# Seven products for the gate and up matmuls of 12 of 22 feature tiles

## The chip, the cores and the metric

One NeuronCore of a Trainium2 chip runs the whole kernel. Its engines work side by side and wait for each other by semaphores: TensorE (PE; PEld is its weight load), VectorE (DVE), ScalarE (ACT), GpSimd (POOL), and SP, whose queue issues most DMA transfers. The metric is the device time of one execution in microseconds; a lower number is better. SBUF is the on-chip memory that all engines read, PSUM the banks that TensorE writes its sums to; a bank holds 128 x 512 numbers of 32 bits.

## What is computed

A decoder trunk of two layers over 512 tokens of width 1024, in 32-bit floats. Each layer is a half-step feed-forward, three gated token mixers side by side, and a second half-step feed-forward, each between RMS norms:

```python
def _swiglu(t, w_gate, w_up, w_down):
    return (jax.nn.silu(t @ w_gate) * (t @ w_up)) @ w_down
for l in range(DEPTH):
    f = _swiglu(_rmsnorm(h, ffn1_pre_g[l]), ffn1_w_gate[l], ffn1_w_up[l], ffn1_w_down[l])
    h = h + 0.5 * _rmsnorm(f, ffn1_post_g[l])
    ...                       # stick-breaking, forgetting and memory attention, gated and merged
    f = _swiglu(_rmsnorm(h, ffn2_pre_g[l]), ffn2_w_gate[l], ffn2_w_up[l], ffn2_w_down[l])
    h = h + 0.5 * _rmsnorm(f, ffn2_post_g[l])
```

The gate and up weights are 1024 x 2816, that is 22 feature tiles of 128 columns; the down weights are 2816 x 1024. There are four feed-forwards, which the tile names call a0, c0, a1 and c1 (the digit is the layer); the mixing stages are b0 and b1.

## The kernel before, in words

**Arithmetic.** A 32-bit product is made of three products of a faster, shorter format. `split` writes a high part of a tile with ScalarE (L188, or L191 with a scale) and the remainder with VectorE (L189, L192); `mm3` (L214 to L216) adds high x high, high x low and low x high into one PSUM bank. So each weight tile costs one DMA, one ScalarE cast and one VectorE subtraction ahead of its matmuls, all in units of 128 x 1024 numbers (512 KB).

**Queue of jobs.** The work for TensorE is a list of jobs, each with the weight units that it needs. When a job begins, its units and the next four are loaded (`load`, `load_ahead`, `AHEAD = 4`); the raw tiles go through a ring of two buffers (tag `raw`), the high and low parts through four each (`wh`, `wl`). `weave` lets TensorE work through jobs while a chain of other steps (normalization, attention heads) waits for its own results; the waits in the attention heads are written as numbers of us (`W_SB0`, `W_SB1`, `W_MORE`). The framework's scheduler then orders the instructions on each engine, and assigns buffers and semaphores; each engine executes its own list strictly in order.

**A feed-forward** (`ffn`). `src.us` is the normalized input, transposed so that features lie on partitions, in high and low parts, for 512 tokens. For feature tiles two at a time: `gates` and `ups` multiply the weight columns (held in the array) with all 512 tokens (streamed), eight k tiles each, so 2 x 2 x 8 x 3 = 96 matmuls of 512 columns for a pair; `hidden` applies SiLU with ScalarE and multiplies with VectorE (L652). The first pair is computed in two halves of the tokens (`halved`, L677 to L680), because the last tokens are normalized late. PSUM has four banks of tag `mm` for these and four of tag `z`.

**The down projection** of the first 16 feature tiles is made with Strassen's seven products instead of eight block products (in Winograd's form, so that sums can be built up step by step), in two chunks of eight tiles: `first_factor` builds sums of blocks of the hidden values, `BlockUnit` loads blocks of the weights and builds their sums on VectorE (L335 to L346) in tiles that `Keep` holds, `product` runs one of the seven (24 matmuls, activations held in the array, weights streamed, output token-major) and copies or adds the PSUM sums into the output tiles (L753, L755). These products are queued one at a time between the gate and up jobs of later tiles. The last six tiles are done in full in `down`, which ends with the residual addition (L598), the next normalization (L605) and the transposes into the next `us` (L615) token tile by token tile.

**The residual stream** `h` is four tiles of 128 x 1024 of tag `o` (eight buffers). It stays in SBUF through a feed-forward; in the mixing stage it is written to a DRAM tensor `hsave` and read back in time for the residual addition.

Of the kernel before, what the change touches and what calls it, by code (L numbers as in the profile page):

```python
# [17 lines left out]
P = 128  # L18
# [4 lines left out]
def kernel(  # L23
# [264 lines left out]
    class BlockUnit(Unit):  # L288
# [19 lines left out]
        def block(self, dst, b):  # L308
            r = (b[0] * self.rows + self.k0) * P
            return nc.sync.dma_start(dst, self.src[r:r + self.nk * P, b[1] * self.ncol:(b[1] + 1) * self.ncol]  # L310
                                     .rearrange("(k p) c -> p k c", p=P))
# [14 lines left out]
        def load(self):  # L326
# [7 lines left out]
            elif self.n == 2:  # L334
                nc.vector.tensor_tensor(t, t, self.raw[:], ALU.subtract)  # L335
                src = t
            elif self.n == 3:
                nc.vector.tensor_tensor(t, b, t, ALU.subtract)
                src = t
            elif self.n == 4:  # L340
                src = b
            elif self.n == 5:
                nc.vector.tensor_tensor(b, b, self.raw[:], ALU.subtract)
# [289 lines left out]

    def ffn(l, src, wg, wu, wd, dst, name, spare, aside=None):
# [7 lines left out]
        tags = ["q"] * 2 + ["o"] * 4  # L642
        act = lambda k, c=FULL: quad_act(src.us)(k, c)

        def hidden(f, pg, pu):
            s = tmp(f"s{name}_{f}")
            nc.scalar.activation(s[:], pg[:], AF.Silu)
            if f < NC * FC:
                i = 2 * f // FC
                if f % (FC // 2) == 0:  # L650
                    hr[i] = stile([P, FC // 2, S], ("k", "tri")[f // FC], f"hr{name}_{i}", F32)
                nc.vector.tensor_tensor(hr[i][:, f % (FC // 2)], pu[:], s[:], ALU.mult)  # L652
                return
            nc.vector.tensor_tensor(s[:], pu[:], s[:], ALU.mult)
            hid[f] = blk(tags[f - NC * FC], f"hid{name}_{f}")
            split(hid[f][:, 0], hid[f][:, 1], s[:])
            if f == NF - 1:
                tc.keep_in_program_order(nc.scalar.preload_act_table_set("natural_log_exp_and_others"))

        def halved(f, ug, uu, half):  # L660
            if half == 0:
                st["p"] = [pbank("mm", f"p{x}{name}_{f + m}") for x in "gu" for m in range(2)]
            else:
                Q.hold, Q.pinned = False, True
                Q.load_ahead()
                Q.pinned = False
            c = HALVES[half]
# [38 lines left out]
        def first_factor(ci, n):  # L706

            a = lambda i, j: hr[2 * ci + j][:, :, HALVES[i]]
# [4 lines left out]
            s = st.get(("s", ci))  # L713
            if n == 2:
                nc.vector.tensor_tensor(s, a(1, 0), a(1, 1), ALU.add)
            elif n == 3:
                nc.vector.tensor_tensor(s, s, a(0, 0), ALU.subtract)
            elif n == 4:
                nc.vector.tensor_tensor(s, a(0, 1), s, ALU.subtract)
            elif n == 5:  # L720
                nc.vector.tensor_tensor(s, a(0, 0), a(1, 0), ALU.subtract)
            src = (a(0, 0), a(0, 1), s, s, s, s, a(1, 1))[n]
            split(h, l, src, scale=-1.0 if n == 6 else None)
# [7 lines left out]
        def product(ci, n, uns):  # L731
            if n == 0 and ci == 0:
                dst.begin()
            if n < 6:
                first_factor(ci, n + 1)
# [21 lines left out]
        def products(ci):  # L757

            def make(i, k0):

                if ci == 0:
                    return stile([P, 2, S], "qo"[i], f"bt{name}_{i}_{k0}", F32)[:]
# [5 lines left out]
            for n in range(7):  # L768
# [4 lines left out]
        for f in range(0, NF, 2):  # L773
            ug = wpair(wg[l], ND, f * P, f"g{name}_{f}")
            uu = wpair(wu[l], ND, f * P, f"u{name}_{f}")
            if f == 0:
# [4 lines left out]
                Q.add([], lambda ug=ug, uu=uu: halved(0, ug, uu, 1), src.ready(range(NT)))  # L781
                marks["first"] = len(Q.jobs)
                continue
            ci = f // FC if f % FC == FC - 2 and f < NC * FC else None
            Q.add(ug, lambda f=f, ug=ug: gates(f, ug))
            for one in todo:
                Q.add(*one)
                break
            if ci is not None:
                Q.add([], lambda ci=ci: iter(first_factor(ci, 0) or ()))  # L790
# [767 lines left out]
```

## Time and profile before

| | |
|---|---|
| time of the kernel, median of 3 runs | 2432.78 us (2432.51 to 2433.62) |
| the profiled execution's own time | 2433.56 us |
| its span, first to last instruction | 2431.8 us |
| granted TensorE clock, mean | 0.999 |
| TensorE busy | 2420.0 us, 11832 matmuls |
| VectorE busy | 1549.7 us |
| ScalarE busy | 1173.6 us |
| GpSimd busy | 78.0 us |
| moved by DMA | 280.46 MB |
| feed-forward a0, from its first matmul to the mixing stage | about 12 to 390 us |
| mixing stage b0 | about 390 to 867 us |
| feed-forward c0 | 867 to 1220 us |
| feed-forward a1 | 1220 to 1596 us |
| mixing stage b1 | 1596 to 2073 us |
| feed-forward c1 and the end | 2073 to 2431 us |

The busy time of TensorE overstates its work, because the profile shows each matmul longer than the distance to the next one; distances between starts are the better measure. A group's row gives line, engine, operation, output and inputs by the program's names, the shape, the count, then total busy us and mean ns, then the idle time of the engine just before and what ended it. A row of the timeline gives start in us, duration in us, engine, line, operation and tiles.

### The profile page before, as it was taken

How to read it: one execution, taken by the hardware profiler on the slowest of the kernel's cores; microseconds unless marked ns; L12 is line 12 of the kernel's file. 1: busy time of each engine (PE TensorE's matmuls, PEld its weight loads, DVE VectorE, ACT ScalarE, POOL GpSimd, SP SyncE). 2: the span in 40 equal slices, each digit the busy share in tenths (PEclk: the TensorE clock that was granted, in tenths of full speed). 3: DMA queues.
4: the chain of work that ended last, by engine and by line, in shares of the span. 5: the costliest groups of instructions: out<-in, count | busy, mean ns of one | idle time of the engine just before them, and what ended most of it. 6: DMA issues, size and time to landing. Idle time of an engine off the chain costs nothing.

```text
span 2431.8 us, 30227 instructions
## 1 busy us (share of the span) xinstructions
PE 2420.0 (100%) x11832; PEld 2044.3 (84%) x11832; DVE 1549.7 (64%) x2183; ACT 1173.6 (48%) x1895; POOL 78.0 (3%) x130
## 2 busy tenths in 40 slices
PE   9999999999999999999999999999999999999998
PEld 8888888888888898888898888888888888888887
DVE  5364677678776654646654546776777866445466
ACT  4333365577655543333433333555775655333333
POOL 0000000001110000000000000000011100000000
PEclk9999999999999999999999999999999999999999
DMA  4334445222223433333424344442232234333433
GB/s 140 116 127 130 133 162 156 70 74 74 87 63 121 138 104 113 130 127 124 156 87 136 109 144 132 159 136 67 73 89 77 79 130 132 94 130 111 141 114 129
DMA packets 234643, 280.46 MB, mean 115 GB/s; under 512 B 8682, under 2 KB 180994, under 8 KB 234500
## 3 DMA queue, kind: packets, MB, share of 16 engines
q1 hardware_dynamic: 234400, 278.50, 35.9%
q8 instruction: 93, 1.52, 0.3%
q14 instruction: 50, 0.41, 0.1%
q0 software_dynamic: 96, 0.03, 0.0%
q10 hardware_dynamic: 4, 0.00, 0.0%
HBM read 272.20 MB, written 6.29 MB: 115 GB/s over the span
## 4 chain that ended last, share of the span: by engine, by line
PE 95%; DVE 2%; ACT 1%; DMA 0%; issue 0%; DVEq 0%; ACTq 0%
PE pg L214 3%; PE pg L215 3%; PE pg L216 3%; PE pgc L215 3%; PE puc L215 3%; PE pgc L214 3%; PE pgc L216 3%; PE puc L214 3%; PE puc L216 3%; PE pga L214 3%; PE pga L215 3%; PE pga L216 3%; PE pdc L214 3%; PE pdc L215 3%; PE pdc L216 3%; PE pda L216 3%
## 5 line engine op out<-in xcount | busy, mean ns | idle before, releaser
L214 PE MATMUL pg<-us_a,wh_wg 128*128 128x512 f32 x384 | 150.6, 392 | 0.0
L216 PE MATMUL pg<-us_a,wl_wg 128*128 128x512 f32 x384 | 149.6, 390 | 0.0
L215 PE MATMUL pg<-us_a,wh_wg 128*128 128x512 f32 x384 | 149.6, 390 | 0.0
L214 PE MATMUL pgc<-us_b,wh_gc 128*128 128x512 f32 x320 | 124.5, 389 | 0.0
L215 PE MATMUL pgc<-us_b,wh_gc 128*128 128x512 f32 x320 | 124.5, 389 | 0.0
L216 PE MATMUL pgc<-us_b,wl_gc 128*128 128x512 f32 x320 | 124.5, 389 | 0.0
L214 PE MATMUL puc<-us_b,wh_uc 128*128 128x512 f32 x320 | 124.5, 389 | 0.0
L215 PE MATMUL puc<-us_b,wh_uc 128*128 128x512 f32 x320 | 124.5, 389 | 0.0
L216 PE MATMUL puc<-us_b,wl_uc 128*128 128x512 f32 x320 | 124.5, 389 | 0.0
L189 DVE TENSOR_TENSOR wl_uc<-raw_uc,wh_uc 128x1024 fp32r<-128x1024 f32 x44 | 53.9, 1225 | 106.6 <-ACT wh_uc L188 106.6
L189 DVE TENSOR_TENSOR wl_ua<-raw_ua,wh_ua 128x1024 fp32r<-128x1024 f32 x44 | 53.8, 1225 | 99.1 <-ACT wh_ua L188 99.1
L188 ACT CAST wh_uc<-raw_uc 128x1024 fp32r<-128x1024 f32 x44 | 46.3, 1052 | 88.5 <-PE pgc L215 37.5
L189 DVE TENSOR_TENSOR wl_gc<-raw_gc,wh_gc 128x1024 fp32r<-128x1024 f32 x40 | 48.8, 1224 | 62.1 <-ACT wh_gc L188 61.8
L216 PE MATMUL pda<-wh_da,ala 128*128 128x512 f32 x224 | 87.1, 389 | 0.0
L214 PE MATMUL pda<-wh_da,aha 128*128 128x512 f32 x224 | 87.1, 389 | 0.0
L215 PE MATMUL pda<-wl_da,aha 128*128 128x512 f32 x224 | 87.1, 389 | 0.0
L214 PE MATMUL pdc<-wh_dc,ahc 128*128 128x512 f32 x224 | 87.1, 389 | 0.0
L215 PE MATMUL pdc<-wl_dc,ahc 128*128 128x512 f32 x224 | 87.1, 389 | 0.0
L216 PE MATMUL pdc<-wh_dc,alc 128*128 128x512 f32 x224 | 87.1, 389 | 0.0
L189 DVE TENSOR_TENSOR wl_ga<-raw_ga,wh_ga 128x1024 fp32r<-128x1024 f32 x40 | 48.8, 1224 | 58.9 <-ACT wh_ga L188 58.8
L188 ACT CAST wh_ua<-raw_ua 128x1024 fp32r<-128x1024 f32 x44 | 46.1, 1051 | 82.0 <-PE pga L215 35.8
L216 PEld LDWEIGHTS pg<-us_a,wl_wg 128*128 128x128 f32 x384 | 72.1, 188 | 15.2
(468 smaller groups left out, 7145.4 us busy)
## 6 DMA issues: line engine op xcount, KB each, us to landing
raw_da<-in_ffn_w_down_dram SPq DMA_DIRECT2D x58, 512.0 KB, 3.7
raw_dc<-in_ffn_w_down_dram SPq DMA_DIRECT2D x58, 512.0 KB, 3.3
raw_wg<-in_w_gate_dram SPq DMA_DIRECT2D x48, 512.0 KB, 3.5
raw_ga<-in_ffn_w_gate_dram SPq DMA_DIRECT2D x44, 512.0 KB, 3.7
raw_ua<-in_ffn_w_up_dram SPq DMA_DIRECT2D x44, 512.0 KB, 3.7
raw_gc<-in_ffn_w_gate_dram SPq DMA_DIRECT2D x44, 512.0 KB, 3.6
raw_uc<-in_ffn_w_up_dram SPq DMA_DIRECT2D x44, 512.0 KB, 3.6
raw_wo<-in_w_out_dram SPq DMA_DIRECT2D x24, 512.0 KB, 3.2
```

The costliest lines, as they stand in the source:

```text
L188: both = [nc.scalar.copy(h_ap, src)]
L189: make = lambda: nc.vector.tensor_tensor(l_ap, src, h_ap.bitcast(F32), ALU.subtract)
L214: nc.tensor.matmul(pt, lh, rh, start=start, stop=False, skip_group_check=free)
L215: nc.tensor.matmul(pt, lh, rl, start=False, stop=False, skip_group_check=free)
L216: nc.tensor.matmul(pt, ll, rh, start=False, stop=stop, skip_group_check=free)
```

## The change

In each feed-forward, feature tiles 2 to 5, 6 to 9 and 14 to 17 (`TG`) are no longer computed by `gates` and `ups`. For a group of four, the gate columns and the up columns (512 each) are put side by side as one matrix of 1024 x 1024, and the product with the tokens (512 x 1024) is made with the same seven products (`group`, `gate_up`): tokens are held in the array, weights streamed, and the result is token-major. The order of the seven is 0, 2, 3, 4, 5, 1, 6, now in the down projection too.

- The sums of weight blocks for these groups are made on GpSimd (`self.engine`); those of the down projection stay on VectorE.
- The sums of blocks of the input are made once per feed-forward (`sums`): two by GpSimd during the first half of the first pair, the others by VectorE in the second half, and split into high and low parts (`parts_of`).
- After the seven products, SiLU and multiplication are done token-major, and `feature_major` transposes the result back with TensorE (16 transposes a group), queued behind the second job of the next group or behind the next gate job.
- The hidden values for the down projection lie in eight tiles of two feature tiles each (`pair`, `HR`), so `first_factor` works in halves of 512 numbers where it took 1024.
- The residual stream is parked in `hsave` at the start of each feed-forward (`park`; for the first one the input `x` itself is read again) and reloaded when the down projection of the last tiles begins (`reload`), which frees four `o` buffers for the kept weight tiles.
- The down products are queued two at a time; `W_MORE` has other numbers.

```diff
@@ class BlockUnit
-        def __init__(self, n, src, rows, k0, nk, ncol, keep, name):
+        def __init__(self, n, src, rows, k0, nk, ncol, keep, name, pair=None):
+            self.pair, self.engine = pair, nc.vector if pair is None else nc.gpsimd
...
             elif self.n == 2:
-                nc.vector.tensor_tensor(t, t, self.raw[:], ALU.subtract)
+                self.engine.tensor_tensor(t, t, self.raw[:], ALU.subtract)
             elif self.n == 3:
-                nc.vector.tensor_tensor(t, b, t, ALU.subtract)
+                self.engine.tensor_tensor(t, b, t, ALU.subtract)
...
             else:
-                nc.vector.tensor_tensor(t, t, self.raw[:], ALU.subtract)
+                ins = (t, self.raw[:]) if self.pair is None else (self.raw[:], t)
+                self.engine.tensor_tensor(t, *ins, ALU.subtract)
@@ before ffn
+    TG = (2, 6, 14)
+    HR = ("q", "q", "o", "o", "rs", "o", "o", "o")
+    ORDER = (0, 2, 3, 4, 5, 1, 6)
@@ in ffn
+        def whole(i, j):
+            t = st["r", i, j] = stile([P, 4, S // 2], "f", f"r{name}_{i}{j}", F32)
+            (nc.vector if i else nc.gpsimd).tensor_tensor(t[:], src.us[j][:, :, 0, HALVES[i]].bitcast(F32),
+                                                          src.us[j][:, :, 1, HALVES[i]].bitcast(F32), ALU.add)
+        def block_sum(n, to, a, b, op, tag):
+            r = st["r", to // 10, to % 10][:]
+            nc.vector.tensor_tensor(r, *(st["r", x // 10, x % 10][:] for x in (a, b)), op)
+            st["a", n] = r, tag
+        def parts_of(n):
+            r, tag = st["a", n]
+            t = stile([P, 2, 4, S // 2], tag, f"ag{name}_{n}")
+            split(t[:, 0], t[:, 1], r)
+            st["ag", n] = t
+        def sums(step):
+            if step == 0:
+                whole(0, 0)
+                whole(0, 1)
+            elif step == 1:
+                whole(1, 0)
+                whole(1, 1)
+                block_sum(2, 11, 10, 11, ALU.add, "k")
+                parts_of(2)
+                block_sum(5, 10, 0, 10, ALU.subtract, "tri")
+                block_sum(3, 0, 11, 0, ALU.subtract, "k")
+                parts_of(3)
+                block_sum(4, 1, 1, 0, ALU.subtract, "tri")
+        def gate_up(f, n, uns):
+            if n in (0, 1, 2):
+                st["gb", SUM[n]] = [pbank("mm", f"pt{name}_{f}_{n}_{e}") for e in range(2)]
+            pts = st["gb", SUM[n]]
+            opens, ends = n in (0, 1, 2), n in (1, 4, 6)
+            for un in uns:
+                for k in range(un.nk):
+                    kk = un.k0 + k
+                    for e in range(2):
+                        mm3(pts[e][:], *input_block(n, kk, e), un.h[:, k], un.l[:, k], opens and kk == 0,
+                            ends and kk == ND // 2 - 1, free=True)
+                        yield 3 * S * PE_US
...
+            for e in range(2):
+                if n == 6:
+                    nc.scalar.activation(t[:, e], pts[e][:], AF.Silu)
+                elif n in (0, 2, 3):
+                    nc.scalar.copy(t[:, e], pts[e][:])
+                else:
+                    nc.vector.tensor_tensor(t[:, e], t[:, e], pts[e][:], ALU.add)
+            if n == 1:
+                nc.scalar.activation(t[:], t[:], AF.Silu)
+            if n in (1, 6):
+                u = st["c", i, 1]
+                nc.vector.tensor_tensor(u[:], u[:], t[:], ALU.mult)
+        def feature_major(f):
+            for i in range(2):
+                u = st.pop(("hid", f, i))
+                for b in range(2):
+                    f2 = f + 2 * b
+                    pt = pbank("z", f"th{name}_{f2}_{i}")
+                    for m in range(2):
+                        for e in range(2):
+                            nc.tensor.transpose(pt[:, (2 * m + e) * P:(2 * m + e + 1) * P],
+                                                u[:, e, (2 * b + m) * P:(2 * b + m + 1) * P], ident[:])
+                    yield 0.45
+                    if f2 < NC * FC:
+                        nc.scalar.copy(pair(f2)[:, :, HALVES[i]], out_)
+                        continue
...
+        def park():
+            if src.name != "x":
+                for t in range(NT):
+                    nc.sync.dma_start(hsave[t], hT[t][:])
@@ the loop over feature tiles
+            if f in TG:
+                some(7)
+                *jobs, turn = group(f)
+                for i, job in enumerate(jobs):
+                    Q.add(*job)
+                    if f == TG[0] and i < 2:
+                        Q.add([], lambda n=ORDER[i + 3]: iter(parts_of(n) or ()))
+                    if i == 1:
+                        behind()
+                later.append(turn)
+                f += 4
+                continue
...
+                Q.add([], lambda: iter(park() or ()))
...
+        def reload():
+            new_h(name)
+            for t in range(NT):
+                nc.sync.dma_start(hT[t][:], hsave[t] if src.name != "x" else x[0, t * P:(t + 1) * P, :])
+        down(wd[l, f0 * P:], NF - f0, hact, down_out, f"d{name}", dst, marks, reload)
```

More of the change, by code (lines that the diff above doesn't have):

```diff
@@ L666, in halved @@
                 Q.pinned = False
+                sums(1)
             c = HALVES[half]
@@ L734, in product @@
             if n < 6:
[L735 removed]
+                first_factor(ci, ORDER[ORDER.index(n) + 1])
             if n in (0, 1, 2):
@@ L772, in ffn, with behind, some @@
         marks, todo = {}, iter(())
-        for f in range(0, NF, 2):
+        later = []
+        def behind():
+            for job in later:
+                Q.add(*job)
+            later.clear()
+        def some(n):
+            for one in itertools.islice(todo, n):
+                Q.add(*one)
+        f = 0
+        while f < NF:
+            if f in TG:
+                some(7)
+                *jobs, turn = group(f)
+                for i, job in enumerate(jobs):
+                    Q.add(*job)
+                    if f == TG[0] and i < 2:
[5 more added lines that the diff above has]
+                continue
             ug = wpair(wg[l], ND, f * P, f"g{name}_{f}")
```

109 lines of the change are left out of this document (71 added, 38 removed).

## The prediction

> **What bounds the kernel now.** I read the page's head first (span, engines, chain), then TensorE's own waits, then a stretch of its timeline.
>
> ```profile
> span 2431.8 us, 30227 instructions
> PE 2420.0 (100%) x11832; PEld 2044.3 (84%) x11832; DVE 1549.7 (64%) x2183; ACT 1173.6 (48%) x1895; POOL 78.0 (3%) x130
> PE 95%; DVE 2%; ACT 1%; DMA 0%; issue 0%; DVEq 0%; ACTq 0%
> ```
>
> ```profile
> PE pts L996 <- ACT ts L1027: 2.2, 4, 0.6
> PE warm L1428 <- DVE warm L1512: 1.3, 1, 1.3
> PE mt L906 <- DVE fa L755: 0.5, 1, 0.5
> PE pga L680 <- ACT us_x L191: 0.4, 1, 0.4
> PE pga L680 <- ACT w_ga L188: 0.2, 1, 0.2
> ```
>
> The second fence is everything TensorE waited for (total us, times, longest): 4.6 us in the whole span. The chain that ended last is TensorE too, 95%. So every matmul taken away is its full pitch gained, as long as nothing new makes TensorE wait; the other engines have room on average (DVE 64%, ACT 48%), and what matters is the stretch into which the new work falls. The profiled execution took 2433.56 us against a median of 2432.78: the sum below is made on 2433.56 and is 0.8 us high against the median. A difference under 0.2% (4.9 us) I count as no change.
>
> **Matmuls removed.** For four feature tiles, gate and up are today 8 column tiles x 8 k x 3 = 192 matmuls of 512 columns; by seven products they are 7 x 4 k x 2 x 3 = 168. Three groups in each of four feed-forwards make 12 groups and 288 matmuls fewer; the built program counts the same (2304 out, 2016 in). Their price is the distance between starts (columns: start, duration, engine, line), since the durations overlap; between these two rows stand the 24 matmuls of one product of the down projection, which has the form of the new ones (weights streamed, activations held):
>
> ```profile
> 310.53 0.39 PE L214 MATMUL pda<-wh_da,aha 128*128 128x512 f32 x1
> ...
> 315.97 0.39 PE L214 MATMUL pua<-us_x,wh_ua 128*128 128x512 f32 x1
> ```
>
> 5.44 / 24 = 0.2267 us. Gain: 288 x 0.2267 = 65.3 us.
>
> **Transposes added.** The token-major results are turned back: 16 per group, 192 in all, on TensorE's path. Eight of them in one row, and the group's mean:
>
> ```profile
> 1620.00 1.03 PE L1110 MATMUL ptm<-ident,pm 128*128 128x128 f32 x8
> ```
>
> ```profile
> L1110 PE MATMUL ptm<-ident,pm 128*128 128x128 f32 x64 | 8.3, 272 | 0.0
> ```
>
> (1.03 - 0.27) / 7 = 0.109 us apart: 192 x 0.109 = 20.9 us lost. Net of both: 44.4 us, or 2389.2, if nothing waits.
>
> **The load of a group on the other engines.** A group takes TensorE 168 x 0.2267 + 16 x 0.109 = 39.8 us. Prices from the groups (busy total, mean ns):
>
> ```profile
> L189 DVE TENSOR_TENSOR wl_uc<-raw_uc,wh_uc 128x1024 fp32r<-128x1024 f32 x44 | 53.9, 1225 | 106.6 <-ACT wh_uc L188 106.6
> L755 DVE TENSOR_TENSOR fc<-fc,pdc 128x512 f32<-128x512 f32 x40 | 26.6, 683 | 8.6 <-PE pdc L216 8.5
> ```
>
> ```profile
> L188 ACT CAST wh_uc<-raw_uc 128x1024 fp32r<-128x1024 f32 x44 | 46.3, 1052 | 88.5 <-PE pgc L215 37.5
> L753 ACT COPY fc<-pdc 128x512 f32<-128x512 f32 x16 | 9.3, 583 | 5.0 <-PE pdc L216 5.0
> ```
>
> VectorE: 14 weight splits (8 before) x 1.225 + 6 PSUM additions x 0.683 + 2 products of 128x1024 x 1.225 = 23.7 us. ScalarE: 14 casts x 1.052, 12 copies or SiLUs of 512 x 0.583, one SiLU of 1024 at about 1.05: 22.8 us. Both fit under 39.8, so by themselves they cost nothing; the matmul stream is their cover.
>
> GpSimd: 8 weight sums per group (two each for products 2, 3, 5, 6). No two-input operation of GpSimd is in the trace. The nearest row is its one-input copy of 1024 elements:
>
> ```profile
> L1237 POOL CAST k<-k 64x1024 fp32r<-64x1024 f32 x16 | 17.6, 1102 | 92.5 <-DVE k L189 78.1 <-ACT ts L1027 10.1 <-issue 4.3
> ```
>
> At least one pass, 1.04 us in its undisturbed instances; with one pass per input 2.08. I take 2.08, since both inputs are full tiles: 16.6 us per group. A gain is excluded, as nothing of it was there before. The Trainium skill (GPSIMD Engine Reference, section 3.1) gives 4497 ns for a two-input add of 2048 elements, against 2293 on VectorE, and its section 4.1 says elementwise work belongs on VectorE; half of that is an estimate of 2.25 us, by which the whole sum below would come to about 2425. No run shows it yet.
>
> **Do GpSimd and VectorE run side by side?** The trace says no, both ways:
>
> ```profile
> 585.40 1.23 DVE L189 TENSOR_TENSOR wl_wb<-raw_wb,wh_wb 128x1024 fp32r<-128x1024 f32 x1 [1.21 <-ACT wh_wb L188]
> 585.93 1.17 POOL L1041 CAST qk<-q 64x512 fp32r<-64x512 f32 x1 [22.84 <-ACT q L191]
> 636.01 0.61 POOL L1041 CAST qk<-q 64x512 fp32r<-64x512 f32 x1 [1.40 <-PE zf L1061]
> 596.99 3.03 POOL L1239 CAST k<-k 64x512 fp32r<-64x512 f32 x1 [9.75 <-ACT k L188]
> 487.28 1.54 POOL L1237 CAST k<-k 64x1024 fp32r<-64x1024 f32 x1 [10.14 <-DVE k L189]
> 487.90 1.20 DVE L203 TENSOR_SCALAR ga<-ga 128x512 f32<-128x512 f32 x1
> ```
>
> A copy of 0.61 us takes 1.17 when it meets a weight split, and ends 0.47 us after that; one took 3.03. The VectorE operation beside the copy at 487.28 took 1.20, and ended 0.28 us after it. So the two take turns. If all of a group's work took turns, 23.7 + 16.6 = 40.3 us against TensorE's 39.8: 0.5 us short per group. Splits run one or two products ahead, so a shortfall can also vanish: 0 at best; at worst every sum costs the 3.03 of that waiting copy, 8 x 3.03 + 23.7 = 47.9, 8.1 us short. I take 0.5 for the 8 groups that are not the first of a feed-forward: 4 us.
>
> **The first group of a feed-forward.** It also needs the block sums of its own input (10 VectorE operations of 1024 elements and two GpSimd ones). The start of the second feed-forward, VectorE and TensorE:
>
> ```profile
> 880.36 1.29 DVE L192 SCALAR_TENSOR_TENSOR us_b<-utb,us_b 128x512 fp32r<-128x512 f32 x2 [1.70 <-ACT us_b L191]
> 881.77 2.36 DVE L189 TENSOR_TENSOR wl_gc<-raw_gc,wh_gc 128x1024 fp32r<-128x1024 f32 x2
> 887.75 1.23 DVE L189 TENSOR_TENSOR wl_uc<-raw_uc,wh_uc 128x1024 fp32r<-128x1024 f32 x1 [3.62 <-ACT wh_uc L188]
> ```
>
> ```profile
> 891.99 0.40 PE L214 MATMUL pgc<-us_b,wh_gc 128*128 128x512 f32 x1
> ```
>
> The input is whole at 881.65; TensorE leaves the halved tiles at 891.99, runs product 0 (5.44) and wants product 2 at 897.4: 15.8 us. In the changed program's order VectorE has, between, 12 two-input operations of 1024 elements (12 x 1.225) and two products of 512 (2 x 0.68, by the row of 683 ns): 16.1 us, 0.3 too long. The two GpSimd sums of product 2 fall in the same stretch; their raw tiles can be fetched only when product 0's splits free the ring (about 884 and 885), and a load of this size lands late:
>
> ```profile
> bta<-in_ffn_w_down_dram SPq DMA_DIRECT2D x16, 512.0 KB, 4.7
> raw_gc<-in_ffn_w_gate_dram SPq DMA_DIRECT2D x44, 512.0 KB, 3.6
> ```
>
> So about 889: they take their turns with a full VectorE queue, 2 x 2.08. ScalarE has its cast of that sum ahead of the SiLU that frees product 0's second bank, so product 0 may wait too; the same delay. First-group wait: 0.3 if GpSimd hides, 0.3 + 4.2 = 4.5 if it takes turns, about 8 if product 3's sum and one more split squeeze in ahead. I take 4.5, x 4 = 18 us. GpSimd's two input sums run in the half before, where VectorE was 11.83 of 20 us busy: nothing, with up to 2 us each if they hold up the last normalization.
>
> ```profile
> 867.00:887.00 20.00, 20.00 (x169) 19.96 (x168) 11.83 (x20) 10.32 (x21) 0.00 (x0) 1.00 0.19 58
> 887.00:907.00 20.00, 20.00 (x110) 17.40 (x110) 6.19 (x6) 5.46 (x7) 0.00 (x0) 1.00 0.32 101
> ```
>
> (PE, PEld, DVE, ACT, POOL busy, clock, DMA share, GB/s.) The second row is where the first group goes: VectorE had 6.19 of 20 us there, now over 12.
>
> **The rest.** Down products now stand in pairs beside the ordinary tiles: per pair and gate job (96 matmuls, 21.8 us) VectorE has 6 weight splits and 2.3 weight sums at 1.225, some 4.5 us of input factors in halves of 512 and 2.7 of PSUM additions (4 x 0.683): about 17.5 us. It fits; 0 to 16 us over all, I take 2. The new product order (0, 2, 3, 4, 5, 1, 6) puts a product between two uses of each PSUM bank, which covers the evictions (0.58); without the cover each would cost 1.2 (two copies). DMA: 72 more weight loads, 12 more stores and 16 more loads of the residual, 100 x 0.52 = 52 MB on 280: no bound. On SP's queue the parked stores stand ahead of product 2's loads and wait only for the last residual addition, some 18 us before need; the reload is read a whole down projection later. Both cost nothing unless that addition is late; then product 2's loads are late with it. Moved waits in the attention heads: at most the 2.2 us of the PE row above either way, taken as 0.
>
> **Sum.** -65.3 + 20.9 + 18 + 4 + 2 = -20.4: 2433.6 - 20.4 = 2413.2 us.
>
> **The rivals.**
> First, all is hidden: the splits run far enough ahead that neither engine's turns matter. For it: VectorE idled 3.62 us in the quoted boundary row. Against it: the 16.1 us in 15.8. 2389 to 2402.
> Second, the other side: VectorE and GpSimd, taking turns, become the bound of the groups. The place is each weight sum ahead of its cast; the price 8 x 3.03 + 23.7 = 47.9 a group. 4 x 8 + 8 x 8.1 = 97 us lost: 2433.6 - 44.4 + 97 = 2486. It decides from 44.4 / 12 = 3.7 us per group, that is from (39.8 + 3.7 - 23.7) / 8 = 2.5 us per sum with full turns. For it: the 3.03 row; against it: that copy met a run of small operations, and VectorE idles in a group for 16 us.
> Third, the clock. TensorE's last matmul began at 2424.38, and the granted clock of the last stretch is below 1:
>
> ```profile
> 2424.38 0.28 PE L216 MATMUL pdc<-wh_dc,hidc 128*128 128x256 f32 x1
> ```
>
> ```profile
> 2423.00:2427.00 4.00, 1.66 (x14) 1.45 (x13) 3.43 (x12) 1.51 (x6) 0.00 (x0) 1.00 0.34 131
> 2427.00:2432.00 5.00, 0.00 (x0) 0.00 (x0) 1.50 (x3) 0.00 (x0) 0.00 (x0) 0.72 0.29 105
> ```
>
> If 0.72 means half clock for 0.56 of the 4.8 us left, the drop came about 4.4 us after the last matmul. A wait of 4.5 us could just do that; a like stretch of 4.4 us at half clock then costs 2.2 us more, four times 9: 2422. The Trainium skill (TensorE: Matmul & The Clock Gate, Part 1) states this rule: an idle window of about 3.4 us halves the clock. The trace agrees at its tail alone.
>
> **Chances and range.** Forecast (2403 to 2420) 0.47; all hidden 0.22; clock 0.10; turns as the bound 0.20; a wash 0.01. Faster: 0.47 + 0.22 and half of the clock's, 0.74; within 0.2%: the rest of the clock's and the wash, 0.06; slower 0.20. The range goes from the bare matmul sum, 2389, to 2442, where each sum takes about 2.55 us in full turns and some of the second rival is inside; the forecast's own range stands above.
>
> **What the new profile would show.** Right: 288 matmuls fewer at the same pitch, 192 transposes at 0.11; TensorE's waits under 30 us, the longest before product 2 of first groups, on VectorE's input sums or the splits of kt; GpSimd's sums near 2.1 us, longer where they meet splits. Wrong: sums of 3 us or more, waits spread over all groups, a granted clock below 1 inside the span, or TensorE idle in the stretches with down products.

## The result, and the profile after

The changed kernel takes 2468.74 us (median of 4 runs, 2466.75 to 2470.49) against 2433.2 us of the kernel before in the runs beside it: ratio 1.0146 (95% interval 1.0128 to 1.0163). It is 1.5% slower; 2413 had been forecast, with 2442 as the upper end. The profiled execution took 2466.75 us.

The head of the changed kernel's profile, its engine line, and the shares of the chain that ended last:

```profile
span 2465.0 us, 30955 instructions
PE 2401.0 (97%) x11736; PEld 2013.9 (82%) x11736; DVE 1820.2 (74%) x2431; ACT 1312.9 (53%) x2133; POOL 363.1 (15%) x234
PE 9%; DVE 1%; DMA 0%; POOL 0%; ACT 0%; issue 0%; DVEq 0%; ACTq 0%; POOLq 0%
```

TensorE has 96 instructions fewer (11832 before: 288 matmuls out, 192 transposes in), but is busy 97% instead of 100%. What it waited for (total us, times, longest):

```profile
PE pta L215 <- DVE wl_ta L189: 13.7, 11, 1.7
PE ptc L215 <- DVE wl_tc L189: 9.1, 7, 2.8
PE ptc L214 <- DVE hrc L656: 9.0, 2, 5.1
PE utc L618 <- DVE fc L608: 5.6, 2, 3.5
PE pta L214 <- DVE hra L656: 5.1, 1, 5.1
PE pta L214 <- ACT wh_ta L188: 2.0, 1, 2.0
```

Before, all of TensorE's waits were 4.6 us; these six rows alone are 44.5. pta and ptc are the banks of the new groups, and nearly every releaser is VectorE: late low halves of weights (wl), and the late product of the halved tiles (hra, hrc), which has to leave its banks before product 2 can open them. GpSimd is named nowhere, although it does the new sums. Its groups by form (count, busy us, mean ns), and below them VectorE's splits of the same blocks and of raw ones:

```profile
L340 POOL TENSOR_TENSOR ktc<-ktc,ktc 128x1024 f32<-128x1024 f32 x12 | 38.2, 3190 | 11.6 <-DVE wl_tc L189 11.6
L345 POOL TENSOR_TENSOR kta<-kta,raw_ta 128x1024 f32<-128x1024 f32 x12 | 33.5, 2804 | 28.6 <-DVE wl_ta L189 25.0 <-issue 3.6
L337 POOL TENSOR_TENSOR ktc<-ktc,raw_tc 128x1024 f32<-128x1024 f32 x12 | 33.0, 2754 | 242.7 <-DMA raw_tc<-in_ffn_w_gate_dram 227.1 <-PE ptc L215 15.5
L349 POOL TENSOR_TENSOR ktc<-raw_tc,ktc 128x1024 f32<-128x1024 f32 x12 | 28.6, 2397 | 46.9 <-DMA raw_tc<-in_ffn_w_gate_dram 46.8
L189 DVE TENSOR_TENSOR wl_tc<-ktc,wh_tc 128x1024 fp32r<-128x1024 f32 x60 | 111.6, 1863 | 67.0 <-ACT wh_tc L188 66.5
L189 DVE TENSOR_TENSOR wl_tc<-raw_tc,wh_tc 128x1024 fp32r<-128x1024 f32 x24 | 29.1, 1221 | 3.6 <-ACT wh_tc L188 3.4
```

A sum takes 2.40 us in product 6 (L349), where nothing disturbs it, and 3.19 on average in product 3 (L340). The forecast had 2.08. A VectorE split takes 1.22 us as ever where its block is raw, but 1.86 on average in the row of kept blocks, 48 of whose 60 GpSimd made. Why, the timelines of the two engines show, at the start of the third feed-forward (start us, us, engine, line, operation; VectorE first, then GpSimd):

```profile
1261.84 5.90 DVE L684 TENSOR_TENSOR ra<-ra,ra 128x1024 f32<-128x1024 f32 x3
1267.66 3.42 DVE L189 TENSOR_TENSOR aga<-ra,aga 128x1024 fp32r<-128x1024 f32 x1
...
1272.14 1.21 DVE L189 TENSOR_TENSOR aga<-ra,aga 128x1024 fp32r<-128x1024 f32 x1
1273.27 3.36 DVE L189 TENSOR_TENSOR wl_ta<-kta,wh_ta 128x1024 fp32r<-128x1024 f32 x1
1276.55 1.21 DVE L684 TENSOR_TENSOR ra<-ra,ra 128x1024 f32<-128x1024 f32 x1
1277.69 1.28 DVE L656 TENSOR_TENSOR hra<-pua,sa 128x512 f32<-128x512 f32 x2
1278.88 2.20 DVE L189 TENSOR_TENSOR wl_ta<-kta,wh_ta 128x1024 fp32r<-128x1024 f32 x1
```

```profile
1263.35 6.65 POOL L337 TENSOR_TENSOR kta<-kta,raw_ta 128x1024 f32<-128x1024 f32 x2 [19.02 <-DMA raw_ta<-in_ffn_w_gate_dram]
1272.29 3.25 POOL L340 TENSOR_TENSOR kta<-kta,kta 128x1024 f32<-128x1024 f32 x1 [2.30 <-DVE wl_ta L189]
1276.71 3.29 POOL L340 TENSOR_TENSOR kta<-kta,kta 128x1024 f32<-128x1024 f32 x1 [1.16 <-DVE wl_ta L189]
```

The GpSimd stretches end at 1270.00, 1275.54 and 1280.00; the VectorE operations that started inside them end at 1271.08, 1276.63 and 1281.08: 1.08 to 1.09 us later each time, nearly the whole of their 1.22. (The three block sums of 1261.84 would take 3 x 1.22 = 3.7 us and took 5.90.) So such a VectorE operation, with both inputs in SBUF, does nothing while it meets a running sum, until the sum is over, and then runs. It is the same throughout the trace: 62 VectorE operations of 128x1024 began inside a sum and ended 1.06 to 1.10 us after it; in two more cases it was the sum that waited, until the VectorE operation was over. It holds the other way too: the sum of 1276.71 met an operation that ended at 1277.76, and took 3.29 instead of 2.40. One kind passes: the two products hra, one of whose inputs is in PSUM, ran in the middle of that sum, 1.28 us for the two, no longer than elsewhere. The Trainium skill (SBUF — State Buffer, "Who interferes with whom") has this as a rule: a VectorE instruction with two SBUF inputs and a GpSimd instruction that reads SBUF exclude each other for the whole instruction, one with at most one SBUF input, outside certain two-port modes, does not contend. These rows agree with both halves of it.

The hra products are ready to run once the halved tiles' last matmul is done, but stand in VectorE's queue behind two splits that wait for GpSimd (1267.66 and 1273.27). TensorE waits 5.08 us for them, and then pays once more:

```profile
1278.42 0.79 PE L214 MATMUL pta<-wh_ta,aga 128*128 128x512 f32 x1 [5.08 <-DVE hra L656]
```

```profile
1279.01 0.63 PE L215 MATMUL pta<-wl_ta,aga 128*128 128x512 f32 x1
...
1283.28 0.55 PE L216 MATMUL pta<-wh_ta,aga 128*128 128x512 f32 x1
```

From 1279.01 to 1283.28 are 10 matmuls, 0.427 us apart instead of 0.227. The same 40 us by engine (us; PE, PEld, DVE, ACT, POOL busy; granted clock; DMA share; GB/s):

```profile
1260.00:1280.00 20.00, 14.93 (x93) 13.15 (x93) 19.83 (x13) 8.22 (x9) 13.19 (x4) 0.92 0.56 185
1280.00:1300.00 20.00, 20.00 (x82) 16.34 (x81) 15.66 (x12) 10.48 (x13) 4.80 (x2) 0.91 0.26 79
```

VectorE shows 19.83 of 20 us busy with 13 operations, of which much is standing still; the granted clock is below 1 although TensorE never paused in the second row.

**Where the time went.** A group loses what lies between its first matmul start and the next start behind its last one, beyond 168 x 0.2267 us (and 16 x 0.109 where transposes stand inside). The figures given here are about 0.1 us per group below these plain distances, which add up to 60.4 us for the twelve instead of 59.3. All that is lost is fixed by the spans: 2465.0 - 2431.8 = +33.2 us where -44.4 was due, so 77.6; what lies outside the groups is the remainder.

| | forecast, us | measured, us |
|---|---|---|
| first groups, 4 | 18 | 30.4 (8.4, 7.1, 7.8, 7.1) |
| the other 8 groups | 4 | 28.9 (second ones 4.0 to 5.5, third ones 1.6 to 4.1) |
| outside the groups | 2 | 18.3 (half of it the transposes of the normalized stream, ut) |
| all | 24 | 77.6 |

How a group's loss reads in rows: the first group of the third feed-forward runs from 1267.61 to the next group's start at 1313.62, 46.0 us for 168 x 0.2267 = 38.1, so 7.9 by these two starts.

### The profile page after: what moved, and what is told of

It is laid out like the page before. It is cut to its first block, busy times and chain, and to the rows that moved or that the text cites. A ratio compares the mean times of both kernels' runs of the same rounds, so it can differ in the third digit from the quotient of the medians.

```text
span 2465.0 us, 30955 instructions
## 1 busy us (share of the span) xinstructions
PE 2401.0 (97%) x11736; PEld 2013.9 (82%) x11736; DVE 1820.2 (74%) x2431; ACT 1312.9 (53%) x2133; POOL 363.1 (15%) x234
## 5 line engine op out<-in xcount | busy, mean ns | idle before, releaser
L189 DVE TENSOR_TENSOR wl_ta<-kta,wh_ta 128x1024 fp32r<-128x1024 f32 x60 | 107.3, 1793 | 82.6 <-ACT wh_ta L188 82.1
L189 DVE TENSOR_TENSOR wl_tc<-ktc,wh_tc 128x1024 fp32r<-128x1024 f32 x60 | 111.6, 1863 | 67.0 <-ACT wh_tc L188 66.5
L188 ACT CAST wh_ta<-kta 128x1024 fp32r<-128x1024 f32 x60 | 62.7, 1050 | 124.0 <-POOL kta L349 39.5
L188 ACT CAST wh_tc<-ktc 128x1024 fp32r<-128x1024 f32 x60 | 62.9, 1051 | 117.8 <-POOL ktc L349 38.5
L215 PE MATMUL pta<-wl_ta,aga 128*128 128x512 f32 x192 | 78.4, 408 | 9.5 <-DVE wl_ta L189 9.3
L214 PE MATMUL ptc<-wh_tc,agc 128*128 128x512 f32 x192 | 76.8, 400 | 9.0 <-DVE hrc L656 9.0
L214 PE MATMUL pta<-wh_ta,aga 128*128 128x512 f32 x192 | 78.2, 407 | 7.1 <-DVE hra L656 5.1
L215 PE MATMUL ptc<-wl_tc,agc 128*128 128x512 f32 x192 | 76.9, 401 | 7.0 <-DVE wl_tc L189 7.0
L215 PEld LDWEIGHTS pg<-us_a,wh_wg 128*128 128x128 f32 x384 | 72.2, 188 | 14.0
L214 PEld LDWEIGHTS pg<-us_a,wh_wg 128*128 128x128 f32 x384 | 72.1, 188 | 14.0
L192 DVE SCALAR_TENSOR_TENSOR wl_wg<-raw_wg,wh_wg 128x1024 fp32r<-128x1024 f32 x48 | 58.6, 1221 | 30.4 <-ACT wh_wg L191 30.3
L216 PE MATMUL pta<-wh_ta,aga 128*128 128x512 f32 x192 | 77.2, 402 | 0.0
```

The costliest lines, as they stand in the source:

```text
L188: both = [nc.scalar.copy(h_ap, src)]
L189: make = lambda: nc.vector.tensor_tensor(l_ap, src, h_ap.bitcast(F32), ALU.subtract)
L192: make = lambda: nc.vector.scalar_tensor_tensor(l_ap, src, scale, h_ap.bitcast(F32), ALU.mult, ALU.subtract)
L214: nc.tensor.matmul(pt, lh, rh, start=start, stop=False, skip_group_check=free)
L215: nc.tensor.matmul(pt, lh, rl, start=False, stop=False, skip_group_check=free)
L216: nc.tensor.matmul(pt, ll, rh, start=False, stop=stop, skip_group_check=free)
```

## Experiments

All are edits of the changed kernel unless another is named. In each, "groups lose" is reckoned as above.

**1. The weight sums on VectorE.**

```diff
-            self.pair, self.engine = pair, nc.vector if pair is None else nc.gpsimd
+            self.pair, self.engine = pair, nc.vector
```

> The changed kernel with its 96 weight sums on VectorE instead of GpSimd; nothing else differs. In the profile of the changed kernel a sum took 2.4 to 3.2 us and a split of a summed block 1.8 (1.22 elsewhere), and the 12 groups lost 59 us against their bare matmuls. Theory 1 (GpSimd's slow sums and the turns are the cause): VectorE gets 8 x 1.225 = 9.8 us per group more, 33.5 of TensorE's 39.8, but splits fall back to 1.22: the loss of second and third groups (4 to 5 and 1.6 to 4 us) falls under 1 each, that of first groups (7.1 to 8.4) to 3 or 4: 59 to about 18, so 2468.7 - 41 = about 2428, between 2418 and 2436. Theory 2 (VectorE's queue in the first groups, with the sums of their own input, is the cause): two more operations there make it worse, first groups lose 7 to 10 each, only the other eight gain: 2445 to 2455. Theory 3 (neither, but the order and the parking): as the changed kernel, 2460 to 2475.

2420.78 us (2420.53 to 2421.89), 0.9951 of before (0.9936 to 0.9966). The groups lose 8.0 us instead of 59: first ones 2.3, 1.8, 0.7, 0.8. The place where 96 additions are made is worth 48 us, and turns a loss into a gain. Theory 2 (VectorE's own queue) falls: VectorE has more to do and the first groups lose less. Theory 1 gave the time within its range, but was too pessimistic on the first groups.

**2. No addition on GpSimd at all**: the two input sums of the halved tiles go to VectorE too.

```diff
-            (nc.vector if i else nc.gpsimd).tensor_tensor(t[:], src.us[j][:, :, 0, HALVES[i]].bitcast(F32),
+            nc.vector.tensor_tensor(t[:], src.us[j][:, :, 0, HALVES[i]].bitcast(F32),
```

> As the run before, and the two sums of the halved tiles' first input half on VectorE too: no GpSimd addition is left in the feed-forwards. Those two GpSimd sums took 2.4 to 3.3 us in the changed kernel, and TensorE's transposes of the normalized stream waited some 9 us in all around them. If these waits come from them (theory 1), this is 4 to 8 us below the run before; if from VectorE's load there (theory 2), 2 x 1.225 us more on it makes it 0 to 6 us slower than the run before.

2407.60 us (2407.47 to 2410.93), 0.9899 of before (0.9885 to 0.9914): 1.0% faster than the kernel before, 2.5% faster than the changed one. Its engine line, TensorE's longest waits, and VectorE's splits and sums of the blocks:

```profile
PE 2382.2 (99%) x11736; PEld 2007.7 (83%) x11736; DVE 1836.4 (76%) x2535; ACT 1314.0 (55%) x2133; POOL 74.3 (3%) x130
PE 80%; DVE 9%; DMA 5%; ACT 3%; issue 2%; POOL 0%; DVEq 0%; ACTq 0%; SPq 0%
```

```profile
PE utc L618 <- DVE fc L608: 2.6, 2, 1.3
PE ptc L214 <- DVE hrc L656: 1.6, 2, 1.4
PE pta L215 <- DVE wl_ta L189: 1.5, 3, 0.8
```

```profile
L189 DVE TENSOR_TENSOR wl_tc<-ktc,wh_tc 128x1024 fp32r<-128x1024 f32 x60 | 72.1, 1221 | 13.5 <-ACT wh_tc L188 13.0
L340 DVE TENSOR_TENSOR ktc<-ktc,ktc 128x1024 f32<-128x1024 f32 x12 | 14.5, 1218 | 0.1
```

VectorE makes 104 additions more than the changed kernel's does, 127 us of work at 1.22, and is busy 16 us longer only: the other 111 had stood there as blocked time. The wait for hra is gone, wl_ta fell from 13.7 us to 1.5, and no split takes longer than 1.23. The eight input sums alone were worth 13.2 us, more than the 4 to 8 expected: the first group of the kernel begins 2.3 us earlier, where a GpSimd input sum had taken 3.3 us, and most of the rest is gained in the stretches that lead from there to the first group of the second feed-forward (5.7 us) and from the third feed-forward's first group to the fourth's (4.2). Which waits these stretches shed was not taken apart.

**3. The weight sums left out.** The lines with the sums are skipped for the groups.

> The changed kernel with the 96 weight sums of the groups left out: products 2, 3, 5 and 6 multiply by single blocks, so the output is not the reference's; every load, split and matmul stays. Theory 1: as with the sums on VectorE or better, as VectorE has 23.7 us of work in a group of 39.8: second and third groups lose under 0.5, first ones 2 to 3: 2415 to 2425. Theory 2: the first groups keep their 7 to 8 us: 2435 to 2445. Theory 3: 2460 or more.

2410.95 us (2 runs). Eleven of the twelve groups keep TensorE's bare pitch within 0.02 us; only the kernel's first one loses 1.0, with a wait of 0.7 us for the halved tiles' product (hra). So without sums nearly every wait in the groups is gone. Beside experiment 1, which has the same GpSimd input sums, the 96 sums on VectorE cost 9.8 us; on GpSimd 57.8.

**4. The kernel before, its down-projection sums on GpSimd**: the 64 additions of lines 335 to 346 of the kernel before, and nothing else.

```diff
-                nc.vector.tensor_tensor(t, b, t, ALU.subtract)
+                nc.gpsimd.tensor_tensor(t, b, t, ALU.subtract)
```

(and so for the three other sums)

> The kernel before with one thing changed: the 64 weight sums of its down products (lines 335 to 346) go to GpSimd. No group, no parking, no other order. Theory 1: each sum takes 2.4 us alone and up to 3.2 beside two-input VectorE work, and VectorE's splits of those blocks go from 1.22 to about 1.8; VectorE is lighter by 64 x 1.225 = 78 us, but the sums arrive later; the down products stand between tiles with slack, so 0 to 15 us slower: 2433 to 2448, with sums of 2.4 us and more in the trace. Rival (a sum costs about 2.08 us and is slowed only by the crowd of the first groups): sums at 2.0 to 2.2, no slower split, 2431 to 2434.

2437.22 us (2436.27 to 2438.59), ratio 1.0017 (1.0007 to 1.0027). Its sums, and its splits of kept blocks (32 of these 40 summed by GpSimd) and of raw ones:

```profile
L346 POOL TENSOR_TENSOR bta<-bta,raw_da 128x1024 f32<-128x1024 f32 x8 | 19.1, 2398 | 50.3 <-DMA raw_da<-in_ffn_w_down_dram 50.3
L338 POOL TENSOR_TENSOR btc<-btc,btc 128x1024 f32<-128x1024 f32 x8 | 23.0, 2894 | 22.8 <-DMA btc<-in_ffn_w_down_dram 22.8
L189 DVE TENSOR_TENSOR wl_dc<-btc,wh_dc 128x1024 fp32r<-128x1024 f32 x40 | 65.3, 1633 | 59.9 <-ACT wh_dc L188 59.7
L189 DVE TENSOR_TENSOR wl_dc<-raw_dc,wh_dc 128x1024 fp32r<-128x1024 f32 x34 | 41.6, 1223 | 47.5 <-ACT wh_dc L188 47.5
```

The same price of 2.40 us alone and 2.9 beside VectorE, and the same blocked splits (1.63 against 1.22), in the old code. Here 64 of them cost 3.9 us in all. That fits the place of the down products, between ordinary tiles with room, but the room was not varied by itself. The rival's 2.0 to 2.2 us per sum is not there.

**5. Which sums harm.** The base is experiment 2; half of the weight sums go back to GpSimd: those of products 5 and 6, or those of 2 and 3, or of 6 alone.

```diff
-            self.pair, self.engine = pair, nc.vector
+            self.pair, self.engine = pair, nc.gpsimd if pair is not None and n in (5, 6) else nc.vector
```

> The changed kernel with the input sums and the weight sums of products 2 and 3 on VectorE; those of products 5 and 6 (48 of 96) stay on GpSimd. With none on GpSimd the time was 2407.6 and the groups lost 7.5 us in all; with all on GpSimd 59. Theory A (throughput: VectorE's two-input work and GpSimd's sums take turns, and their sum has to fit into TensorE's 39.8 us of a group): 23.7 + 4 x 1.225 + 4 x 2.4 = 38.2 us, or 39.8 with 2.8 us per sum: it just fits, groups lose 8 to 20 us in all, 2408 to 2420, whichever products keep their sums there. Theory B (latency: each sum ends 1.2 us or more later ahead of its cast, and the early products of a group have the least lead): the late products have the lead, 2407 to 2412.

> The mirror image: the weight sums of products 2 and 3 (48 of 96) on GpSimd, those of 5 and 6 and the input sums on VectorE. The same work for the two engines together. Theory A (throughput): the same time as its mirror image within 4 us, 2408 to 2420. Theory B (latency of the early products): half the sums keep most of the loss: first groups lose 5 to 7, the others 2 to 4 each, 40 us in all: 2430 to 2445.

> The version without GpSimd additions (2407.6) with the sums of product 6 alone (24 of 96) on GpSimd. They are the last of a group; where products 5 and 6 were there (2421.0), those of 5 took 3.0 us, those of 6 2.40, with VectorE idle beside them. If harm comes from blocking alone, a place where VectorE idles is harmless and VectorE gains 4.9 us of room in each group: 2404 to 2410. If the second sum of each pair holds up the split of the first one (one split took 2.68 there), a third to a half of the 13.4 us remains: 2411 to 2415.

| weight sums on GpSimd | us | against experiment 2 | groups lose |
|---|---|---|---|
| none (experiment 2) | 2407.6 | | 7.5 |
| product 6, 24 sums | 2412.9 (2412.1 to 2416.9) | +5.3 | 12.0 |
| products 5 and 6, 48 sums | 2421.0 (2418.7 to 2423.8) | +13.4 | 17.3 |
| products 2 and 3, 48 sums | 2449.1 (2448.4 to 2452.3) | +41.5 | 48.5 |
| all, 96 sums (experiment 8) | 2465.8 (2462.3 to 2468.8) | +58.2 | 60.6 |

Theory A, that only the sum of the two engines' work counts, falls: the same 48 additions cost three times as much in products 2 and 3. Theory B had the order right, but was too kind to products 5 and 6 (2407 to 2412 expected). With products 2 and 3 there, TensorE's long waits are those of the changed kernel:

```profile
PE ptc L214 <- DVE hrc L656: 9.0, 2, 5.1
PE pta L215 <- DVE wl_ta L189: 8.8, 7, 1.8
PE ptc L215 <- DVE wl_tc L189: 6.8, 7, 1.5
PE pta L214 <- DVE hra L656: 5.1, 1, 5.1
```

Product 6 is the mildest place; VectorE has idle time there (3.95 us ahead of the first row below). Even so the second sum of each pair blocks the split of the first one: in experiment 5 with products 5 and 6, a sum ran from 922.19 for 2.39 us, and the split that met it took 2.68 (VectorE's row, then GpSimd's):

```profile
922.98 2.68 DVE L189 TENSOR_TENSOR wl_tc<-ktc,wh_tc 128x1024 fp32r<-128x1024 f32 x1 [3.95 <-ACT wh_tc L188]
```

```profile
922.19 2.39 POOL L349 TENSOR_TENSOR ktc<-raw_tc,ktc 128x1024 f32<-128x1024 f32 x1 [0.33 <-DMA raw_tc<-in_ffn_w_gate_dram]
```

**6. Late, or blocked?** A GpSimd sum makes its cast 1.2 us later even if it blocks nobody. Here every sum is on VectorE, and the block is then copied onto itself on ScalarE, so that it is late and nothing is blocked.

```diff
+            if self.pair is not None and self.n in (2, 3, 5, 6):
+                nc.scalar.copy(src, src)
             self.split_from(src)
```

> The version without GpSimd additions (2407.6; groups lose 7.5 us) with one copy more on ScalarE behind every weight sum: the sum on VectorE (1.22), then the block copied onto itself on ScalarE (1.05 us in the trace), then cast and split. So each sum is about as late as GpSimd's alone (1.22 + 1.05 and a handover, against 2.40), and VectorE is never blocked by anyone. Theory B1 (lateness of each sum ahead of its cast is what the groups lose): nearly as with GpSimd, groups lose 35 to 55 us: 2436 to 2456. Theory B2 (it is the blocking: VectorE's two-input work stands still while GpSimd adds, and GpSimd while VectorE works): groups lose 8 to 18 us: 2408 to 2420.

2423.52 us (2421.01 to 2424.71), 0.9958 of before (0.9942 to 0.9975); the groups lose 18.7 us. The copies took 1.05 us each, the splits stayed at 1.22:

```profile
L352 ACT COPY kta<-kta 128x1024 f32<-128x1024 f32 x48 | 50.5, 1054 | 45.2 <-DVE kta L349 28.9 <-DVE kta L337 13.2 <-DVE kta L345 2.0
L189 DVE TENSOR_TENSOR wl_ta<-kta,wh_ta 128x1024 fp32r<-128x1024 f32 x60 | 72.4, 1222 | 23.3 <-ACT wh_ta L188 23.3
```

So lateness of this size, with what 101 us more work on ScalarE costs beside it, is at most 11 of the 53 us that the groups lose by GpSimd's sums (60.6 - 7.5), and at most 15.9 of the 58.2 us of time; the remaining 42 need the blocking. Theory B1 falls. The time is 3.5 us above the upper end given for B2, the groups' loss 0.7.

**7. The clock.** Experiment 2 with four made waits (the first low half of product 2 in each third group passes through GpSimd copies and comes back unchanged).

> The version without GpSimd additions, with four made waits: in the third group of each feed-forward the first low half of product 2 goes through 6, 9, 12 and 15 GpSimd copies of 512 elements and comes back unchanged, so that TensorE waits for it. That operand was whole 3.0 us ahead of its use, and a copy took some 0.6 to 0.8 us, so the waits should be about 1, 3, 5 and 8 us. Theory with the clock (the prediction's third rival): after waits of 4 us and more, 8 to 12 matmuls follow at 0.43 us instead of 0.227, some 2 us more than the wait, and none after a wait of under 3 us. Without it: 0.227 after each wait. Time about 2407 + 17 to 25 = 2424 to 2434.

2453.18 us (one run), 19 us above the range expected; the 45.6 us over experiment 2 lie in the four third groups. The copies took 0.61 to 1.65 us each, 1.17 on average, more than was expected, so the waits came out otherwise than planned: 5.8, 4.2, 3.9 and 7.3 us (the last three with shorter ones just ahead of them). After them 8, 13, 13 and 11 matmuls ran 0.427 us apart. The first, by stretches: the wait, the slow matmuls, the normal ones.

```profile
209.00:215.00 6.00, 0.34 (x2) 0.17 (x2) 5.30 (x4) 2.88 (x5) 5.59 (x4) 0.74 0.32 99
215.00:219.00 4.00, 4.00 (x11) 3.14 (x11) 1.23 (x1) 0.43 (x1) 0.00 (x0) 0.54 0.00 0
219.00:223.00 4.00, 4.00 (x19) 3.30 (x18) 2.34 (x2) 2.41 (x3) 0.00 (x0) 1.00 0.00 0
```

11 matmuls in 4 us at a granted clock of 0.54, then 19 in 4 us at 1.00. So a wait of 4 to 7 us costs 1.6 to 2.6 us beyond itself (8 to 13 x 0.2). Some 43 matmuls of the changed kernel's groups ran at half rate: 8.6 us of the 59.

The waits of this run do not say how short a wait is harmless, and the expectation's 3 us is not a bound. In the changed kernel a wait of 1.73 us (it ended at 94.79) was followed by half clock, and one of 2.78 us (ended at 960.59) was not:

```profile
92.35:95.76 3.41, 1.69 (x7) 1.02 (x6) 3.41 (x2) 1.70 (x3) 2.25 (x2) 1.00 0.90 295
95.76:99.17 3.41, 3.41 (x10) 2.37 (x8) 3.41 (x2) 1.04 (x2) 2.34 (x1) 0.50 0.26 102
...
955.92:959.33 3.41, 1.89 (x8) 1.12 (x6) 3.37 (x2) 1.05 (x1) 3.41 (x2) 1.00 0.53 158
959.33:962.75 3.42, 2.16 (x9) 1.80 (x10) 2.44 (x2) 1.53 (x2) 2.26 (x2) 1.00 0.02 5
962.75:966.16 3.41, 3.41 (x24) 2.92 (x23) 1.02 (x1) 2.10 (x3) 1.28 (x1) 1.00 0.00 0
```

The changed kernel's trace has the granted clock fall at 47.98, 95.76, 914.96, 1249.47, 1276.78 and 2136.93 us, all whole multiples of 3.413 us apart, for 3.41 or 6.83 us each time. In the traces of all these runs, past their first 14 us, the clock fell after such a stretch of 3.41 us in which TensorE's waits added up to 1.67 us or more (26 stretches that had begun at full clock, the last 8 us of each run left out), and never after one with 1.0 to 1.65; between 1.67 and 1.73 both occur. So about half a stretch of idling was enough, and the wait of 2.78 us escaped because it was shared by two stretches, 1.52 and 1.26 us. The Trainium skill (TensorE: Matmul & The Clock Gate, Part 1) puts the idle window at about 3.4 us; the length of the stretches agrees, but TensorE did not have to idle through a whole one.

**8. Smaller suspects.** The input sums alone moved to VectorE; the old list of moved waits (W_MORE) in experiment 2; and, in the kernel before, the parking of the residual stream alone.

> The changed kernel with only the sums of the halved tiles' first input half moved to VectorE; all 96 weight sums stay on GpSimd. Moving these eight sums was worth 13.2 us where the weight sums were on VectorE (2420.8 to 2407.6). If their harm is at the normalization, apart from the groups, it is worth the same here: 2468.7 - 13 = 2453 to 2458. If it only adds to the queue that the first groups wait for anyhow, it is hidden there: 2462 to 2470.

> The version without GpSimd additions (2407.6) with the old list of moved waits in the attention heads (W_MORE as in the kernel before). By the prediction this list is worth 0, at most 2.2 us either way. If the new list was fitted to this order: 2408 to 2412. If the old one was as good: 2406 to 2408.

> The kernel before with the parking alone: after the halved tiles the residual stream is stored (12 stores in three of the four feed-forwards) and read again ahead of the last down projection (16 loads). No groups, no other order. The prediction costs this at 0: the stores stand ahead of weight loads on SP's queue, the reload is read a whole down projection later: 2431 to 2435. If a late store or load holds up weight loads: 2 us for each of the four feed-forwards, 2439 to 2445.

Input sums: 2465.79 us (2462.34 to 2468.84), ratio 1.0133 (1.0117 to 1.0148), not told apart from the changed kernel's 1.0146. What is worth 13.2 us without weight sums on GpSimd is mostly hidden with them. That an earlier start only waits at the same queue would explain it, but was not shown by itself.
Wait list: 2406.68 us (2406.13 to 2407.57), the same as with the new one (2407.47 to 2410.93).
Parking: 2433.79 us, ratio 1.0002 (0.9992 to 1.0011). No cost shows.

## Why the prediction was wrong

- **Matmuls and transposes (-65.3 and +20.9): right.** The counts are those of the forecast, and between two waits the new matmuls keep their pitch; between these rows of the changed kernel lie the last 24 of a group, 5.48 / 24 = 0.228 us; in experiment 3 the second groups, with 16 transposes inside, take 39.62 us from first to last start for 167 x 0.2267 + 16 x 0.109 = 39.60:

```profile
1111.36 0.39 PE L214 MATMUL ptc<-wh_tc,us_b 128*128 128x512 f32 x1
...
1116.84 0.39 PE L214 MATMUL pgc<-us_b,wh_gc 128*128 128x512 f32 x1
```

- **The turns of GpSimd and VectorE, 0.5 us per group: wrong, and this is the step that failed.** The groups lose 59.3 / 12 = 4.9 us each. One part is the price of a sum, 2.08 us, taken as two passes of a one-input copy (2 x 1.04); an addition takes 2.40 alone. The estimate from the Trainium skill's figure (GPSIMD Engine Reference, section 3.1), 2.25, was nearer, and still low. With 2.40 the forecast's own formula gives 23.7 + 8 x 2.40 - 39.8 = 3.1 us short per group instead of 0.5, 37 us over 12 groups, and by this arithmetic alone nearly all of the gain is gone. The other part is the formula, which adds up busy times and holds them against TensorE's 39.8 us. In experiment 5 with products 2 and 3 it gives 23.7 + 4 x 1.22 + 4 x 2.40 = 38.2 us, which fits; with the 2.93 us that its sums took on average, waiting included, it is 40.3, or 0.5 short. The groups lose 48.5 / 12 = 4.0 us each all the same.
- **"The two take turns": right, but its consequence was missed.** The rows show that a whole VectorE queue stands still behind one blocked split, and that what stands there may be something TensorE needs first: the hra and hrc products, which free banks. What is queued behind the waiting instruction was named for ScalarE (its cast ahead of the SiLU), not for VectorE.
- **First groups, 4 x 4.5: the right place, 30.4 us instead of 18.** The forecast's cause, 16.1 us of VectorE work in 15.8, is not it: with all sums on VectorE there is more such work, and these groups lose 2.4, 1.8, 0.6 and 0.7 us (experiment 2). What these groups wait for is the blocked queue (hra, hrc and the low halves), and on top came the half clock.
- **The other 8 groups, 0.5 each: wrong, 3.6 each.** Second groups lose 4.0 to 5.5, third ones 1.6 to 4.1; that second ones inherit the backlog of the first would fit, and was not tested.
- **Input sums, taken as nothing, "up to 2 us each": too low without weight sums on GpSimd**, where eight were worth 13.2 us, 1.65 each and inside the bound given; mostly hidden with them.
- **Wait list and parking, 0: right** (experiment 8).
- **The rest, 2 us: too low.** Outside the groups 18.3 us are lost, and 10.8 even in experiment 2, about half of them in four waits of 1.1 to 1.5 us at the normalizations and the attention stages. Which parts of the new order make them was not taken apart.
- **The rivals.** The second, turns as the bound, was what happened, with 0.20 of the chance. Its price of 3.03 us per sum was too high (2.40 to 3.19 on average by product), hence 2486 instead of 2469; its point of decision, 3.7 us per group, was passed with 4.9. The third, the clock, did occur, on top of the second rather than in its place, which the list of cases did not allow for. That 8.6 us in the groups come so near its 9 is luck: it reckoned with four waits of 4.5 us, and the clock fell at five places in the groups, at two of them behind waits of 2.04 us and less.
- The forecast of 2413 is close to the kernel in which the change does without GpSimd (2407.6), in part by chance: there the groups lose 7.5 us and the rest 10.8, where 22 and 2 had been forecast. The arithmetic on TensorE's side was sound; what failed was the price of helping VectorE out with an engine that stops it.

## What to carry to other kernels

Before work is moved from VectorE to GpSimd, look at what VectorE does in that very stretch: if it is two-input work on SBUF, the move does not add an engine, it exchanges 1.22 us on VectorE for 2.40 us in which VectorE's two-input work stands still. Here 23.7 + 9.8 us on VectorE alone fitted into 39.8, and 23.7 + 19.2 on the two together did not. Reckon such a pair as one engine, but take the sum as a lower bound only (23.7 + 4.9 + 9.6 = 38.2 us fitted as well, and lost 4.0 us a group), and ask what is queued behind the instruction that gets blocked; the harm per sum was 0.06 us in the down products (experiment 4, 3.9 / 64) and 0.86 in products 2 and 3 (41.5 / 48).

## What the runs showed of the hardware that was not expected

The exclusion works both ways: VectorE operations of 128x1024 with both inputs in SBUF that began inside a GpSimd sum ended 1.06 to 1.10 us after it, however long they had waited (62 cases in the changed kernel), and sums that began while such an operation ran took up to 4.47 us instead of 2.40. VectorE operations with one input in PSUM ran through, 1.28 us for two. A GpSimd subtraction of 128x1024 f32 takes 2.40 us undisturbed, VectorE 1.22. TensorE's clock is granted by stretches of 3.41 us on a fixed grid: waits of about half a stretch (1.67 to 1.73 us) were enough to halve it for the next one, for 7 to 13 matmuls of 512 columns at 0.427 us, while a wait of 2.78 us that lay across two stretches left it alone.
